# Silu of c first, gate's products beside the first pair's sums, d_skip turned behind dt, two weight differences moved

## The chip, the cores and the metric

The kernel runs on one core of one Trainium2 chip. The metric is the device time of one execution in microseconds. Three executions of the kernel before took 1301.9, 1305.21 and 1306.17 us; their median, 1305.21 us, is the time before. All times on a profile count from the start of its span.

TensorE is called PE here, VectorE DVE, ScalarE ACT, GpSimd POOL and SyncE SP. PEld is PE's weight load, which overlaps its products. SP computes nothing; its queue issues most of the loads, ACT's queue most of the stores. Each engine takes its instructions in the order in which they are written for it.

## The reference

One decoder layer runs on a prompt of 1024 rows and on 8 samples of 8 rows (64 rows), so on 1088 columns in all, with a model width of 1024:

```
mod = silu(c) @ w_ada + b_ada ; shift, scale, gate = split(mod, 3)
h = rmsnorm(x) * (1 + scale) + shift
[u_pool | z_pool | z_ssm | xBC | dt | g] = h @ w_in
P = (pool_mix(u_pool) * silu(z_pool)) @ w_pool_out
S = gated_rmsnorm(SSD(conv(xBC)) + d_skip * x, z_ssm) @ w_ssm_out
x = x + gate * ((sigmoid(g_pool) * P + sigmoid(g_ssm) * S) @ w_o)
y = rmsnorm(x, final_g)
```

`c` has nine rows: one for the prompt and one for each sample. `w_ada` is 1024 x 3072: its first 1024 columns give shift, the next scale, the last gate. Shift and scale are wanted at once, because h is made with them; gate is wanted only at the very end, when rows of y are made. `d_skip` is one number per head (32 heads) and is wanted by the SSD stage. The outputs are y for prompt and samples and the new pool, convolution and SSM states.

## The kernel before, in words

Everything is held turned: channels on the 128 partitions, the 1088 rows of x along the columns. Products are made in float32 precision by splitting each operand into a high and a low part (`whi`, `wlo`; `hh_`, `hl_`) and summing three products. Most of `h @ w_in` is done two output tiles at a time by a Strassen scheme: a *pair* is seven products, each of two halves of 272 columns, whose operands are sums of quarters of h and of w_in. The sums of h (S1, S2, S3) are made once, by `combine()`; the sums of weights are made for every pair, by `steps()` or, for the first pair, by `first_steps()`.

The change touches the opening, `first()`. There the order of the instructions of PE, ACT, DVE, POOL and SP is written out by hand and kept (`in_line`): each engine runs them as they stand in the text. Its stages are these.

- *Load and norm.* SP loads nine tiles of x (tiles 0 to 7 of 128 rows, tile 8 of the 64 sample rows), then the weights of shift and scale in two parts of eight tiles (`ada_load`: part 0 goes with h tiles 0 to 3, part 1 with 4 to 7), with raw tiles of w_in between them (`w_load`). `x_square` sums the squares of one tile on DVE or ACT, `x_root` takes the root on ACT (Sqrt table), `x_unit` takes the reciprocal and scales each x tile by it on DVE (L211).
- *Turning.* `x_turn(g3, k)` turns channel tile k of a block of x on PE and copies it out on DVE (even k) or ACT (odd k). Block 0 is x tiles 0 and 1 (256 columns), block 1 tiles 2 to 4 (384), block 2 tiles 5 to 8 (448). Block sums live in the same banks of PSUM (pools PA with three banks and PB with five).
- *Shift and scale.* `c_turn` takes Silu of c on ACT (Silu table), turns it on PE and copies it to `scT`. `ada_mm(part, k)` multiplies it with weight tile k, in four column groups of PE at once. When all eight are summed, `ada_end` copies the sum out on ACT, turns it on PE and adds the biases on DVE, into `md`. `v_turn` turns the bias vectors.
- *h and the first two output tiles.* `h_make(block, ks)` writes high and low parts of h for some channel tiles, on ACT and DVE. `products(block, ks)` multiplies them with the weights of two tiles of g by the plain scheme; `done` takes Sigmoid on ACT (Sigmoid table) and stores it.
- *dt and the first pair.* `dt_block` multiplies h by the 32 dt columns (`dtw`), three blocks of 256, 384 and 448 columns; ACT writes the result into one of the buffers `s1`, `u2`, `u3` and stores it. `done` uses the same buffers in the order s1, u2, u3, c2, s1, u2. `combine()` is a generator; each `next(sums)` issues a step on DVE and ACT: four steps of three sums each for S2, with a high part on ACT and the low part of the step before on DVE, then S3, S1 and the fourth operand. `late_loads()` loads the convolution's weights and d_skip and, at its second step, copies d_skip out on DVE (L342) and turns both on PE (L344, L345). Then the first pair (`light[0]`, z columns) runs; between its products a hook issues the next steps of the weight splits (`wst`) and of `combine()`.

Behind `first()` a list of units runs: `light[1]` (a pair of z columns), `gate_unit(0)`, `light[2]`, `gate_unit(1)`, and then sixteen heavy pairs (pool and convolution columns, with much DVE work) into which two more light pairs are woven; then ten light pairs beside the samples' SSD, the prompt's SSD beside the output products, and the tail with w_o. These later parts are ordered by priorities and by simulated times, not by hand.

`gate_unit(half)` makes 512 columns of gate: it loads eight weight tiles of 128 x 512 through four buffers of the unit stage (`GA`), multiplies them with `scT` in four column groups, two weight tiles per group, copies the four partial sums out on ACT and adds them by one more product with `sel9` (L1012), adds the bias on DVE and stores the nine rows to `gate_d` in DRAM.

Buffers that matter: `rawA` (three; raw weights of pairs, squares, the copied-out sums of shift and scale, and dtw), `raw` (three), `R` (three; c, x tile 8, later S1), `sq` (one; later S1's last tile).

## Time and profile before

| what | value |
|---|---|
| median of three executions | 1305.21 us |
| the profiled execution's own time | 1307.45 us |
| its span on the profile | 1305.4 us |
| granted TensorE clock over the span | 0.99 |
| busy time: PE, DVE, ACT, POOL | 1261.2, 899.9, 698.7, 677.9 us |
| DMA moved | 251.66 MB, mean 193 GB/s |

How to read the lines that follow. The page begins with the busy time of each engine; then the span is cut into 40 equal slices, with a digit for the busy tenths of each engine, the clock granted to PE in tenths of full speed, and the rate of DMA. A line of waits names who waited (engine, tile written, line of the program), for whom, the total in us, how often, and the longest. A line of the timeline gives the start and the duration in us, the engine (with a q behind its name: its queue, mostly issuing a DMA), the line, the operation, output and inputs, shapes, how many were merged, and in brackets the idle time of the engine ahead of it with what ended it. Where several are merged the duration is their sum; PE's is from the first start to the last modelled end. A line of a window gives the stretch, its length, the busy time and number of instructions of PE, PEld, DVE, ACT and POOL, then clock, DMA share and GB/s. A line of a group gives count, busy time, mean ns of one, and the idle time before.

### The profile page before, as it was taken

The page shows a single profiled execution, that of the slowest core. Times are in us where ns is not written, and L with a number is a line of the kernel's source. Part 1 is how long each engine was busy: PE and PEld are TensorE (multiplying, and loading weights), DVE is VectorE, ACT ScalarE, POOL GpSimd, SP SyncE. Part 2 cuts the span into 40 slices and gives each one's busy share as a digit, 9 for nine tenths or more (in the row PEclk, how much of TensorE's full clock was granted, in tenths as well). Part 3 has the DMA queues.
Part 4 walks back from the last instruction along what each step waited for, and adds up shares of the span by engine and source line. Part 5 has one row for each costly group of instructions (what it writes and reads, how often), then busy time and mean ns, then how long its engine had stood idle before and what let it go on. Part 6 is the DMA issues. An engine that isn't in the chain of part 4 may idle for free.

```text
span 1305.4 us, 26075 instructions
## 1 busy us (share of the span) xinstructions
PE 1261.2 (97%) x9575; PEld 1159.5 (89%) x9575; DVE 899.9 (69%) x1510; ACT 698.7 (54%) x1661; POOL 677.9 (52%) x564
## 2 busy tenths in 40 slices
PE   4989999999999999999999999999999999999998
PEld 3768899999999999999889899888888888999786
DVE  5676387978967888875777665477675877466533
ACT  4764336555746655545544554676987766201211
POOL 1006567877887877664344453366676756214000
PEclk8989999999999999999999999999999999999999
DMA  9428644645654644444556465999988665475621
GB/s 324 147 79 275 204 131 152 199 131 169 215 167 147 191 159 150 151 133 128 164 153 189 147 177 164 345 360 369 303 284 264 207 197 162 166 268 158 228 98 56
DMA packets 232568, 251.66 MB, mean 193 GB/s; under 512 B 31101, under 2 KB 173573, under 8 KB 232434
## 3 DMA queue, kind: packets, MB, share of 16 engines
q1 hardware_dynamic: 160308, 171.56, 41.5%
q10 hardware_dynamic: 72134, 78.45, 17.7%
q8 instruction: 76, 1.25, 0.4%
q14 instruction: 50, 0.41, 0.1%
HBM read 167.06 MB, written 83.01 MB: 192 GB/s over the span
## 4 chain that ended last, share of the span: by engine, by line
PE 48%; DVE 4%; DMA 4%; POOL 3%; issue 3%; ACT 3%; ACTq 0%; SPq 0%; POOLq 0%; DVEq 0%
PE mm L320 4%; PE mm L321 4%; PE mm L322 4%; PE ps L567 3%; PE ps L568 3%; PE ps L569 3%; PE mm L567 3%; PE mm L569 3%; PE mm L568 3%; PE ps L1831 2%; PE ps L1833 2%; PE ps L1832 2%; PE ps L1157 2%; PE ps L1373 1%; PE ps L1160 1%
## 5 line engine op out<-in xcount | busy, mean ns | idle before, releaser
L163 POOL TENSOR_TENSOR wlo<-rawA,whi 128x512 fp32r<-128x512 f32 x120 | 192.9, 1612 | 189.0 <-ACT whi L160 113.8
L163 POOL TENSOR_TENSOR wlo<-raw,whi 128x512 fp32r<-128x512 f32 x92 | 149.8, 1634 | 127.2 <-ACT whi L160 123.7
L320 PE MATMUL mm<-Y,whi 128*128 128x352 f32 (+1 forms) x480 | 164.7, 343 | 0.5 <-DVE G L1734 0.4
L321 PE MATMUL mm<-Y,whi 128*128 128x352 f32 (+1 forms) x480 | 158.6, 330 | 1.0 <-DVE Y L1408 1.0
L322 PE MATMUL mm<-Y,wlo 128*128 128x352 f32 (+1 forms) x480 | 158.2, 330 | 0.0
L567 PE MATMUL mm<-Y,whi 128*128 128x272 f32 x496 | 147.0, 296 | 0.7 <-DVE GA L583 0.4
L567 PE MATMUL ps<-Y,whi 128*128 128x272 f32 x496 | 144.6, 292 | 0.8 <-DVE h L1253 0.5
L569 PE MATMUL mm<-Y,wlo 128*128 128x272 f32 x496 | 143.1, 289 | 2.0 <-POOL wlo L163 2.0
L568 PE MATMUL mm<-Y,whi 128*128 128x272 f32 x496 | 143.1, 289 | 0.4 <-DVE Y L447 0.4
L568 PE MATMUL ps<-Y,whi 128*128 128x272 f32 x496 | 143.1, 289 | 0.0
L569 PE MATMUL ps<-Y,wlo 128*128 128x272 f32 x496 | 142.8, 288 | 0.0
L160 ACT ACTIVATE whi<-rawA 128x512 fp32r<-128x512 f32 x125 | 78.3, 627 | 106.9 <-PE ps L568 49.9
L965 DVE SCALAR_TENSOR_TENSOR GA<-GA,cvT,GA 128x1112 f32<-128x1112 f32 x72 | 129.8, 1807 | 0.0
L160 ACT ACTIVATE whi<-raw 128x512 fp32r<-128x512 f32 x96 | 58.8, 626 | 92.4 <-DVE raw L514 58.2
L567 PEld LDWEIGHTS mm<-Y,whi 128*128 128x128 f32 x496 | 93.3, 188 | 6.0 <-ACT whi L160 1.7
L320 PEld LDWEIGHTS mm<-Y,whi 128*128 128x128 f32 x480 | 91.3, 190 | 6.6 <-issue 4.3
L567 PEld LDWEIGHTS ps<-Y,whi 128*128 128x128 f32 x496 | 93.3, 188 | 4.1 <-issue 2.7
L569 PEld LDWEIGHTS mm<-Y,wlo 128*128 128x128 f32 x496 | 93.4, 188 | 2.8 <-POOL wlo L163 2.4
L568 PEld LDWEIGHTS mm<-Y,whi 128*128 128x128 f32 x496 | 93.4, 188 | 1.5 <-DVE Y L447 0.8
L568 PEld LDWEIGHTS ps<-Y,whi 128*128 128x128 f32 x496 | 93.3, 188 | 0.3 <-issue 0.2
L569 PEld LDWEIGHTS ps<-Y,wlo 128*128 128x128 f32 x496 | 93.4, 188 | 0.2 <-issue 0.2
L321 PEld LDWEIGHTS mm<-Y,whi 128*128 128x128 f32 x480 | 91.4, 190 | 1.7 <-DVE Y L1408 1.6
(448 smaller groups left out, 3780.1 us busy)
## 6 DMA issues: line engine op xcount, KB each, us to landing
rawA<-in_w_in SPq DMA_DIRECT2D x46, 512.0 KB
dec<-acs_d SPq DMA_DIRECT2D x32, 512.0 KB
xbc<-GA ACTq DMA_DIRECT2D x24, 512.0 KB
xb<-xbc SPq DMA_DIRECT2D x32, 384.0 KB
rawA<-in_w_in SPq DMA_DIRECT2D x32, 256.0 KB
pw<-in_w_ssm_out ACTq DMA_DIRECT2D x32, 256.0 KB
ws<-ph ACTq DMA_DIRECT2D x32, 256.0 KB
ws<-pw SPq DMA_DIRECT2D x32, 256.0 KB
```

What stands on the lines that cost most here:

```text
L160: ins = act(hi[:, :, :ncols], raw[:, :, :ncols], AF.Copy)
L163: (eng or nc.gpsimd).tensor_tensor(lo[:, :, :ncols], raw[:, :, :ncols], hi[:, :, :ncols].bitcast(F32), ALU.subtract)
L320: mm(ps[:, :n], a, rh[k][:, o:o + n], start=(k == 0), stop=False)
L321: mm(ps[:, :n], a, rl[k][:, o:o + n], start=False, stop=False)
L322: mm(ps[:, :n], b, rh[k][:, o:o + n], start=False, stop=(k == nk - 1))
L567: mm(p, hi, ah, start=(k == 0), stop=False)
L568: mm(p, hi, al, start=False, stop=False)
L569: mm(p, lo, ah, start=False, stop=(k == 3))
L965: V.scalar_tensor_tensor(d[:, :n], rp[:, k:k + n], cvT[:, 24 * k + mc:24 * k + mc + 1], d[:, :n], ALU.mult, ALU.add)
L1157: mm(o[hh], xd[:S, 2 * q + hh, :], dec[:S, 2 * q + hh], start=True, stop=state is None)
L1831: mm(ps[:, :cw], mhk, wo[k][0][:, s], start=(k == 0), stop=False)
L1832: mm(ps[:, :cw], mhk, wo[k][1][:, s], start=False, stop=False)
```

## The change

- Silu's table is loaded first, by the small activation that loaded Sqrt's before, now ahead of four small loads of bias vectors. `c_turn` stands behind the first two squares instead of between the turns of the third block.
- x tiles 5 and 6 are scaled on POOL instead of DVE. The square of x tile 7 on DVE and the root of tiles 5 to 7 stand behind the first four turns of block 1.
- The eight shift-and-scale products of part 0 stand between the turns of block 2, and only its last turn is behind `ada_end(0)`.
- `first_steps()` makes its first two differences (t3 and t2) in a step of their own, which runs ahead of `ada_end(1)`; for that the first pair's weights are asked for earlier on SP. `dtw` gets a buffer of its own beside the turned x.
- Gate's products are part of `first()`: eight weight tiles of 128 x 1024 in the buffers R and sq, all eight summed in one bank in four column groups of 256 columns; four behind the later `products` of blocks 0 and 1, four behind the dt blocks. The sum is copied with its bias by one DVE instruction and stored by four DMAs on SP. `gate_unit`, `sel9` and the two units are gone.
- All six `done` run before the sums; the dt blocks follow the `products` directly; the second step of `late_loads` (d_skip) stands behind the dt blocks and gate's last products.
- `light[2]` is woven among the heavy pairs, three light pairs instead of two.

```diff
--- before.py
+++ after.py
@@ -127,14 +127,14 @@
     c9 = R([NB + 1, D])
     store_(c9[0:1, :], c_prompt)
     store_(c9[1:NB + 1, :], c_sample)
+
+    act(rc[:, 0:1], eps, AF.Silu)
+    nc.gpsimd.memset(rc[:, 0:1], 1.0)
     vb = sm.tile([44, P], F32, tag="stc", name="vb", bufs=4)
     store_(vb[0:16, :], b_ada[0, 0:2048].rearrange("(m p) -> m p", p=P))
     store_(vb[16:24, :], norm_g[0].rearrange("(m p) -> m p", p=P))
     store_(vb[24:40, :], ssm_norm_g[0].rearrange("(m p) -> m p", p=P))
     store_(vb[40:44, :], pool_scale[0].rearrange("(m p) -> m p", p=P))
-
-    act(rc[:, 0:1], eps, AF.Sqrt)
-    nc.gpsimd.memset(rc[:, 0:1], 1.0)
     scT = const([P, KT, 32], "scT")
     nc.gpsimd.memset(scT, 0.0)
     vT = const([P, 44], "vT")
@@ -208,7 +208,7 @@
         n = xr[a][1]
         V.reciprocal(rs[:n, a:b], rs[:n, a:b])
         for i in range(a, b):
-            V.tensor_scalar(xr[i][0][:n], xr[i][0][:n], rs[:n, i:i + 1], None, ALU.mult)
+            (nc.gpsimd if i in (5, 6) else V).tensor_scalar(xr[i][0][:n], xr[i][0][:n], rs[:n, i:i + 1], None, ALU.mult)
 
     tf = [None] * KT
 
@@ -515,10 +515,11 @@
 
             def first_steps():
                 t3, t2 = raw_(), raw_()
+                diff(t3, b22, b12)
+                diff(t2, t3, b11, ALU.add)
+                yield
                 add(b11)
                 add(b21)
-                diff(t3, b22, b12)
-                diff(t2, t3, b11, ALU.add)
                 diff(b21, t2, b21)
                 yield
                 add(b21)
@@ -683,7 +684,7 @@
 
 
     def dt_w():
-        raw = pa.tile([P, KT, NH], F32, tag="rawA", name="dtw", bufs=3)
+        raw = tfp.tile([P, KT, NH], F32, tag="dtw", name="dtw", bufs=1)
         load(raw, w_in[0, :, C_DT:C_DT + NH].rearrange("(k p) c -> p k c", p=P))
         return raw
 
@@ -789,6 +790,32 @@
         yield 1
 
 
+    gate_d = dram("gate_d", [NB + 1, D])
+    gw, gp2 = {}, []
+
+    def gate_load(k):
+        gw[k] = hs.tile([P, D], F32, tag="sq", name=nm("gk"), bufs=1) if k % 4 == 3 else R((P, D))
+        load(gw[k], w_ada[0, k * P:(k + 1) * P, 2 * D:])
+
+    def gate_mm(k):
+        if k == 0:
+            gp2.append(PB())
+        for j in range(4):
+            mm(gp2[0][32 * j:32 * j + 32, :256], scT[:, k, :], gw[k][:, 256 * j:256 * j + 256], start=(k == 0), stop=(k == KT - 1))
+
+    def gate_bias():
+        bg = tfp.tile([P, 256], F32, tag="bg", name="bg", bufs=1)
+        nc.gpsimd.memset(bg, 0.0)
+        for j in range(4):
+            load(bg[32 * j:32 * j + NB + 1], b_ada[0, 2 * D + 256 * j:2 * D + 256 * j + 256].partition_broadcast(NB + 1))
+        return bg
+
+    def gate_end(bg):
+        V.tensor_tensor(bg, gp2[0][:, :256], bg, ALU.add)
+        for j in range(4):
+            load(gate_d[:, 256 * j:256 * j + 256], bg[32 * j:32 * j + NB + 1])
+
+
     def first():
         ET = mybir.EngineType
         every = (ET.PE, ET.Activation, ET.DVE, ET.Pool, ET.SP)
@@ -847,6 +874,7 @@
 
         x_square(0, V)
         x_square(1, V)
+        c_turn()
         x_root(0, 2)
         x_unit(0, 2)
         x_square(2, None)
@@ -861,11 +889,11 @@
             x_turn(0, k)
         x_unit(4, 5)
         x_square(5, None)
-        x_square(7, V)
         x_square(6, None)
-        x_root(5, 8)
         for k in range(4):
             x_turn(1, k)
+        x_square(7, V)
+        x_root(5, 8)
         x_unit(5, 8)
         x_square(8, None)
         x_root(8, 9)
@@ -873,23 +901,25 @@
             x_turn(1, k)
         x_unit(8, 9)
         v_turn()
-        for k in range(2):
+        ada_mm(0, 0)
+        for k in range(4):
             x_turn(2, k)
-        c_turn()
-        for k in range(2, 4):
-            x_turn(2, k)
-        for k in range(4):
-            ada_mm(0, k)
+            if k % 2:
+                ada_mm(0, 1 + k // 2)
         w_split(0, 0)
         w_split(1, 0)
-        for k in range(4, 8):
-            ada_mm(0, k)
+        ada_mm(0, 3)
         x_turn(2, 4)
+        ada_mm(0, 4)
+        x_turn(2, 5)
+        ada_mm(0, 5)
+        ada_mm(0, 6)
+        ada_mm(0, 7)
+        x_turn(2, 6)
         ada_end(0)
 
         h_make(0, range(4))
-        for k in range(5, 8):
-            x_turn(2, k)
+        x_turn(2, 7)
         products(0, range(4))
         h_make(1, range(4))
         ada_mm(1, 0)
@@ -901,28 +931,36 @@
         for k in range(2, 8):
             ada_mm(1, k)
         products(2, range(2))
+        dtw = dt_w()
+        run, (wz, wst) = light[0][1], light[0][0]()
+        bg = gate_bias()
+        for k in range(4):
+            gate_load(k)
+        next(wst)
         ada_end(1)
-        dtw = dt_w()
         products(2, range(2, 4))
 
         for bi in range(3):
             h_make(bi, range(4, 8))
         for bi in range(3):
             products(bi, range(4, 8))
-
-        run, (wz, wst) = light[0][1], light[0][0]()
+            for k in range(2 * bi, min(2 * bi + 2, 4)):
+                gate_mm(k)
+                gate_load(k + 4)
+
         next(wst)
-        for bi in range(2):
+        for bi in range(3):
             for t in range(2):
                 done(bi, t)
         sums = combine()
-        next(sums)
-        for t in range(2):
-            done(2, t)
-        next(late, None)
         for i in range(3):
             dt_block(dtw, i)
             next(sums)
+        for k in range(4, 8):
+            gate_mm(k)
+        next(late, None)
+        next(sums)
+        gate_end(bg)
         next(wst)
 
         def hook(n):
@@ -978,41 +1016,6 @@
         store_(new_conv_p[0, 0, :, mc * P:(mc + 1) * P], o27[0:3])
         store_(new_conv_s[0, :, :, mc * P:(mc + 1) * P], o27[3:27])
         yield 1
-
-
-    gate_d = dram("gate_d", [NB + 1, D])
-    sel9 = const([P, NB + 1], "sel9")
-    nc.gpsimd.tensor_tensor(sel9, ident[:, 0:9], ident[:, 32:41], ALU.add)
-    nc.gpsimd.tensor_tensor(sel9, sel9, ident[:, 64:73], ALU.add)
-    nc.gpsimd.tensor_tensor(sel9, sel9, ident[:, 96:105], ALU.add)
-
-    def gate_unit(half):
-        c = slice(2 * D + half * 512, 2 * D + half * 512 + 512)
-
-        def ws():
-            out = []
-            for j in range(4):
-                w = GA([P, 2, 512])
-                load(w, w_ada[0, 2 * j * P:(2 * j + 2) * P, c].rearrange("(k p) c -> p k c", p=P))
-                out.append(w)
-            return out
-
-        def run(w):
-            bg = GA([P, 512])[:NB + 1]
-            load(bg, b_ada[0, c].partition_broadcast(NB + 1))
-            pg = PB()
-            for kk in range(2):
-                for r in range(4):
-                    k = 4 * kk + r
-                    mm(pg[32 * r:32 * r + 32, :], scT[:, k, :], w[k // 2][:, k % 2], start=(kk == 0), stop=(kk == 1))
-            gs = pa.tile([P, 512], F32, tag="c2", name=nm("gs"))
-            act(gs, pg, AF.Copy)
-            yield
-            ps = PB()
-            mm(ps[:NB + 1, :], sel9, gs, start=True, stop=True)
-            V.tensor_tensor(bg, ps[:NB + 1, :], bg, ALU.add)
-            store_(gate_d[:, half * 512:half * 512 + 512], bg)
-        return (ws, run)
 
     H0B = 4
 
@@ -1473,8 +1476,8 @@
             load(new_pool_s[0, :, 0:7, :], state_pool[0, :, 8:15, :])
 
     first()
-    units = [plain(to_conv), light[1], gate_unit(0), light[2], gate_unit(1), plain(pool_rows)]
-    units += weave(heavy, light[3:-LAST])
+    units = [plain(to_conv), light[1], plain(pool_rows)]
+    units += weave(heavy, light[2:-LAST])
     pre = splits()
     units.append(plain(lambda: [None for _ in pre]))
     units.append(plain(to_ssd))
```

## The prediction

> **What bounds the kernel now.** I read the page's busy times and slices first, then TensorE's own waits over the first 130 us, then busy time by stage, then the timeline of the stages that the change touches.
>
> ```profile
> PE 1261.2 (97%) x9575; PEld 1159.5 (89%) x9575; DVE 899.9 (69%) x1510; ACT 698.7 (54%) x1661; POOL 677.9 (52%) x564
> ...
> PEclk8989999999999999999999999999999999999999
> ...
> GB/s 324 147 79 275 204 131 152 199 131 169 215 167 147 191 159 150 151 133 128 164 153 189 147 177 164 345 360 369 303 284 264 207 197 162 166 268 158 228 98 56
> ```
>
> PE (TensorE) is busy 97% of the span, so the time moves only where PE stands still, runs at the lower clock, or gets other work. The clock line shows both dips in the first three slices (32.6 us each). The GB/s line bounds what has landed: 324 GB/s over the first slice is 10.6 MB.
>
> ```profile
> PE ps L345 <- DVE dx L342: 3.8, 1, 3.8
> PE ps L147 <- ACT R L144: 3.0, 1, 3.0
> ```
>
> These are PE's two longest single waits of the first 130 us that the change addresses: for the turned `d_skip` (L345) and for Silu of c (L147).
>
> ```profile
> core 0: us, PE busy (x) PEld busy (x) DVE busy (x) ACT busy (x) POOL busy (x), PEclk, DMA share, GB/s
> 22.70:25.60 2.90, 0.00 (x0) 0.00 (x0) 0.00 (x0) 2.88 (x3) 0.00 (x0) 0.50 1.13 332
> 25.70:32.20 6.50, 6.50 (x48) 3.82 (x52) 0.86 (x2) 1.58 (x3) 2.08 (x2) 0.50 0.89 311
> ...
> 54.00:62.00 8.00, 7.28 (x49) 6.69 (x48) 6.02 (x17) 6.45 (x12) 0.00 (x0) 1.00 0.25 77
> ...
> 68.10:72.10 4.00, 0.16 (x1) 0.16 (x1) 3.65 (x7) 2.00 (x5) 0.00 (x0) 0.77 0.37 131
> 72.10:76.90 4.80, 4.80 (x45) 2.04 (x49) 4.50 (x9) 1.96 (x5) 0.00 (x0) 0.50 0.34 128
> 76.90:82.00 5.10, 5.10 (x60) 1.58 (x52) 4.12 (x6) 1.75 (x3) 0.00 (x0) 0.98 0.20 67
> 200.00:300.00 100.00, 100.00 (x782) 97.98 (x781) 84.79 (x122) 60.76 (x148) 77.48 (x45) 1.00 0.56 174
> ```
>
> Each row has the stretch, its length, the busy time of the five engines, granted clock, DMA share and rate. PE is idle from 22.70 to 25.60, runs to 32.20 at clock 0.50, is idle again from 68.10 to 72.10 and at 0.50 to 76.90. From 200 to 300 it has no idle time at all while DVE has 85: there, whatever is saved ahead passes through to the end.
>
> **The change part by part.** *Start.*
>
> ```profile
> 15.49 1.22 DVE L199 SCALAR_TENSOR_TENSOR sqj<-Y 128x1024 f32<-128x1024 f32 x1 [1.04 <-DMA Y<-in_x_prompt]
> ...
> 21.68 0.27 PE L222 MATMUL ps<-ident,R 64*128 64x64 f32 x1 [1.44 <-DVE R L211]
> ...
> 22.36 0.31 PE L222 MATMUL ps<-ident,R 64*128 64x64 f32 x1
> ...
> 23.26 1.28 ACT L144 ACT_TABLE_LOAD   x1
> ...
> 24.55 1.06 ACT L144 ACTIVATE R<-R 9x1024 f32<-9x1024 f32 x1
> ...
> 26.61 0.90 PE L222 MATMUL ps<-ident,Y 128*128 128x128 f32 x3
> ...
> 27.74 0.90 PE L222 MATMUL ps<-ident,Y 128*128 128x128 f32 x3
> ...
> 28.87 5.53 PE L244 MATMUL ps<-Y,scT 128*32 128x256 f32 x64
> ...
> 36.22 1.09 ACT L283 ACTIVATE Y<-tf,md 128x256 fp32r<-128x256 f32 x2 [1.35 <-DVE md L256]
> ...
> 46.97 2.80 PE L244 MATMUL ps<-G,scT 128*32 128x256 f32 x48
> ```
>
> Before, Silu's table load (1.28) and Silu (1.06) stand behind the second turn of the third block (rows 21.68 and 22.36); two more turns follow at half clock, and the first shift-and-scale product starts at 28.87, the last ends at 34.40, and the first h is written at 36.22. A turn takes 0.68 at full clock (22.36-21.68) and 1.13 at half (27.74-26.61). A shift-and-scale step of one weight tile takes 2.80/6 = 0.47 at full clock, so about 0.9 at half. All eight weight tiles are within the first 9.2 MB of the sync queue (x is 8 loads of 512 KB and one of 256, weights 8 of 512, two raws of 256), which by the rate of the first slice is there at 9.2/0.324 = 28.3 us.
>
> After, the Silu table takes the place of the first Sqrt table, Sqrt is loaded right behind Silu, so there are as many loads as before, and the first root comes between 0 and 1.28+1.06 later; I take 0.6, as most of it lies beside the first vector squares. DVE's wait for x tile 7 (1.04 in row 15.49) swallows that. That square ended at 16.7; behind the first two vector copies of the second block it ends about 1.5 later, so with root and reciprocal the scalings of tiles 5 to 7 start near 18.9. Two of the three go to POOL, where the trace has no scaling by a column. Its bounds:
>
> ```profile
> L163 POOL TENSOR_TENSOR wlo<-rawA,whi 128x512 fp32r<-128x512 f32 x120 | 192.9, 1612 | 189.0 <-ACT whi L160 113.8 <-DVE S L447 66.4 <-PE ps L1247 6.4
> ...
> L1136 POOL TENSOR_SCALAR_AFFINE_SELECT dec<-dec 128x1024 f32<-128x1024 f32 x32 | 36.0, 1125 | 23.5 <-DMA R<-gp 10.2 <-ACT cE L1341 7.1 <-DMA dec<-acs_d 6.0
> ```
>
> One input of 1024 columns took 1.12 us (L1136); two inputs of 512 took 1.61, so 1024 would take 3.2. Two tiles are ready at 21.1 or at 25.3. Nearest is L1136, one input and the same width: 21.1, before the 21.68 at which the third block started anyway, so it costs nothing; its upper end costs 3.6. The Trainium skill (GPSIMD Engine Reference, section Engine selection) says that one-input work on POOL is roughly line-rate and two-input work about twice as slow as VectorE; at the one-input rule the cost stays zero. Its specifications say that POOL shares SBUF interfaces with VectorE instructions in a two-port mode, which speaks against the edit; no run here prices that.
>
> From 21.7 PE then has six turns and seven weight steps until the part is summed: 6x0.68+7x0.47 = 7.4 us at full clock, so 29.1; 13.2 at half, so 34.9, as late as before. With a drop as at 22.3 and a recovery as at 72.10 to 76.90 (4.8 us at half, which cost 2.4) it is 31.5. I take 31.2 against 34.40: **3.2 us gained** (0 to 5.3). The split of the first two raws moves up with the turns, so the raw buffer that held the queue comes free sooner and no later load is held back.
>
> *Two weight differences.*
>
> ```profile
> 52.63 0.20 DVE L256 TENSOR_TENSOR md<-ps,vT 128x36 f32<-128x36 f32 x1 [1.16 <-PE ps L252]
> ```
>
> Two DVE instructions of 0.68 (row 67.47 below) move from behind the first pair's splits to ahead of the second part's sums of shift and scale. DVE idles there for 1.16, waiting for PE's turned sums, so 1.36 cost 0.2, taken as nothing; if the raws are late, see the rivals. `dtw` in a buffer of its own frees a `rawA`, so both raws can load at once.
>
> *Gate's first four products.* 4x0.47 = 1.9 on PE, beside 0.72 of idle time in the row 54 to 62: 1.2 lost. Its eight loads of 512 KB and four bias loads go on SP behind the pair's raws, with a DMA share of 0.25 in that row. The last four wait only for the products that free their buffers; behind them on SP stand the stores of gate, which wait for DVE's gate sum near 80, then the next pair's raws, which are needed only when the first pair's seven products are nearly through.
>
> *d_skip behind dt.*
>
> ```profile
> 66.75 1.28 ACT L830 ACT_TABLE_LOAD   x1
> ...
> 67.47 0.68 DVE L514 TENSOR_TENSOR raw<-rawA,rawA 128x512 f32<-128x512 f32 x1
> ...
> 68.05 0.39 ACT L830 ACTIVATE g<-mm 128x256 f32<-128x256 f32 x1
> ...
> 68.88 0.38 ACT L830 ACTIVATE g<-mm 128x256 f32<-128x256 f32 x1 [0.44 <-ACT g L830]
> ...
> 69.53 0.72 DVE L466 TENSOR_TENSOR tf<-tf,tf 128x544 f32<-128x544 f32 x1
> ...
> 78.91 1.68 PE L697 MATMUL mm<-Y,dtw 128*32 128x448 f32 x16
> ...
> 82.02 0.39 PE L567 MATMUL mm<-Y,whi 128*128 128x272 f32 x1
> ...
> 634.78 0.34 ACTq L681 DMA_DIRECT2D z<-u  x1
> ...
> 638.25 0.44 DVE L578 TENSOR_TENSOR u<-s,mm 128x272 f32<-128x272 f32 x1 [1.78 <-DMA z<-u]
> ```
>
> PE idles 68.1 to 71.9 on DVE's copy of d_skip, and two thirds of dt run at half clock. The last dt block (448 columns) took 82.02-78.91 = 3.11 at full clock; all 1088 columns then take 7.6. With 3.2 gained and 1.2 lost PE ends the block products at 66.1, dt at 73.7, gate's last four products (1.9) at 75.6. That would be 6.4 before 82.02. What is late next is the d_skip copy: DVE has it behind three steps of sums, and the second and third hold a low part that waits for ACT's high part, which stands behind the dt evacuation. That one writes the buffer of the fifth Sigmoid, whose store must land. In numbers: Sigmoids start at 68.05-3.2 = 64.9, one per 0.85, so the fifth's store leaves at 69.0; a store took 3.5 from issue to its reader in the rows at 634.78 and 638.25. Then dt 0.5, gap 0.4, high part 0.7, low part 0.7, three sums (0.72 each), low part 0.7, copy 0.2, turn 0.3: 78.1. With a landing that nobody waits for PE sets it: 75.6. The DMA share is 0.37 or less here (rows 68.10 and 72.10), so I take a landing a little quicker than that, 77.4: the first product of the pair starts **4.6 us** before 82.02 (0.5 to 6.4). This contains the start's gain and all of gate's new PE work.
>
> The Trainium skill (TensorE: Matmul & The Clock Gate, Part 1) says that an idle window of about 3.4 us halves the clock and a busy one restores it, on a free-running window. The trace agrees: 3.85 idle, then 0.50 for 4.8 us. By it the wait left, below 2.5 us, keeps full clock, as I assume.
>
> *Gate units gone.*
>
> ```profile
> 152.25 1.92 PE L1007 MATMUL ps<-GA,scT 128*32 128x512 f32 x16
> 154.10 0.40 PE L567 MATMUL mm<-Y,whi 128*128 128x272 f32 x1
> ...
> 157.57 1.03 PE L1012 MATMUL ps<-gs,sel 128*9 128x512 f32 x2
> 158.53 0.39 PE L567 MATMUL ps<-Y,whi 128*128 128x272 f32 x1
> ```
>
> One half took PE 154.10-152.25 and 158.53-157.57: 1.85+0.96 = 2.81; two halves **5.6 us**, saved whole, since PE has no idle time behind. Also gone are their 4 MB of loads there, two ACT evacuations, and on POOL three tiny sums. The third light pair goes among the heavy ones. Three light pairs spread over sixteen heavy ones instead of two: runs of heavy pairs get shorter, and PE was fully busy in longer ones, so nothing (-3 to +4 for other phases of later waits).
>
> Sum: 4.6+5.6 = 10.2 against the profiled run of 1307.45 (span 1305.4 and 2.05 around it): 1297.2. That run lies 2.2 above the median; against 1305.21 I predict 1295.
>
> **The rivals.** (1) The start gives nothing: PE at half clock throughout, or POOL at 3.2 per tile, or the last weights late. For it: the clock did fall at 22. Against: PE now has unbroken work. 3.2 less: 1298.2. (2) The d_skip copy is only moved into a longer chain on DVE: S2 late by 4 more takes back nearly all of 4.6: 1299. For it: the in-order queue above; against: it needs a landing of over 7 us. (3) Slower: DVE stands in line at the two differences until both raws are there.
>
> ```profile
> 41.73 11.30 SPq L500 DMA_DIRECT2D rawA<-in_w_in  x2
> ```
>
> Before, the second load could leave only at 53 (11.30 for two). After, the queue ahead of them is 15.1 MB, by 0.324 there at 46.6 and needed at 48.0 (52.63, less 3.2, less the two themselves). Each us later delays the second half of h, one for one; 10.2 late is no change, over 14 late is slower: 1310. That requires the second load to wait for a buffer and gate's weights to pass it; SP is in order and gate's loads stand behind. (4) Other waits take it back: of PE's 44 us of idle time (1305.4-1261.2) a part lies in later stages, where its phase moves, and could grow by 8; 1303. Against: the row from 200 to 300.
>
> **How the numbers follow.** Forecast 0.62; (1) 0.15; (2) 0.08; (3) 0.05; (4) 0.10. About 0.3% (3.9 us) is what a measurement of this kernel can tell from no change: faster below 1301.3, slower above 1309.1. The forecast, (1) and (2) are faster, 0.85 in all, of which 0.02 stray to no change; (4) is no change but for 0.01; (3) is slower. So 0.83, 0.11, 0.06. The forecast's own range is 1289 (start 5.3, no wait at d_skip, 2 from later waits) to 1300. To leave out 2 in 10 it runs to 1303, and 1288 below for the scatter of the runs.
>
> **What would show it.** Last part-0 product near 31; PE's wait at L345 below 2.5; dt at clock 1.00 in under 8 us; first pair's first product near 77; the second pair at once followed by the heavy one without gate products. Wrong if the differences wait on DMA, if POOL's scalings last over 2 us each, or if PE's idle time behind 100 us grows by more than 4.

## The result, and the profile after

Twenty executions of the changed kernel have a median of 1303.34 us (1301.43 to 1307.35), twenty of the kernel before, on the same chips, 1304.76 (1301.77 to 1309.53). The ratio is 0.9988 with a 95% interval of 0.9979 to 0.9998: a gain of about 0.1%, where 0.8% was forecast, and just above the range's upper end of 1303. The profiled execution of the changed kernel took 1303.16 us with a span of 1301.4, so it lies at its median, while the profiled execution of before lies 2 to 3 us above its own. Of the 4.2 us between the ends of the two traces less than half is therefore in the medians.

First the head of the page of the changed kernel: busy times, then granted clock of PE in 40 slices of 32.5 us.

```profile
PE 1260.4 (97%) x9603; PEld 1162.7 (89%) x9603; DVE 888.8 (68%) x1507; ACT 698.3 (54%) x1659; POOL 681.0 (52%) x564
...
PEclk8999999999999999999999999999999999999999
```

The second dip (the 8 in the third slice of before) is gone; the first stayed. PE's waits over the first 130 us (who waited, for whom, total, times, longest) and the timeline of the opening say why.

```profile
PE ps L147 <- ACT R L144: 6.4, 1, 6.4
PE ps L222 <- POOL Y L211: 3.9, 2, 2.3
...
PE ps L345 <- DVE dx L342: 0.8, 1, 0.8
```

```profile
19.15 6.22 POOL L211 TENSOR_SCALAR Y<-Y,rs 128x1024 f32<-128x1024 f32 x2 [15.78 <-DVE rs L209]
...
22.14 11.50 SPq L828 DMA_DIRECT2D raw<-in_w_in  x2
...
25.42 0.69 PE L222 MATMUL ps<-ident,Y 128*128 128x128 f32 x2 [2.34 <-POOL Y L211]
...
35.67 1.50 PE L244 MATMUL ps<-Y,scT 128*32 128x256 f32 x24
...
38.99 1.09 ACT L283 ACTIVATE Y<-tf,md 128x256 fp32r<-128x256 f32 x2 [1.37 <-DVE md L256]
```

The two scalings on POOL took 6.22 us, 3.1 each on average, and ended at 25.37; the prediction's own sign of being wrong was over 2 us each. PE waited for the first and again for the second, and could turn the third block in earnest only from 25.42. The last shift-and-scale products of part 0 ended at 37.17 (before: 34.40) and the first h is written from 38.99 (before: 36.22). The two raw loads on SP wait for a buffer that the late turns hold back, so the weights of part 1 behind them are asked for only at 33.69. The 6.4 us wait at L147 is the first 6.4 us of the span, in which PE has nothing else to do.

Windows of the changed kernel (stretch, length, busy time of PE, PEld, DVE, ACT, POOL, clock, DMA share, GB/s):

```profile
21.80:25.40 3.60, 0.48 (x1) 0.18 (x1) 0.77 (x1) 0.00 (x0) 3.57 (x2) 0.50 1.10 337
25.40:35.20 9.80, 9.78 (x53) 4.65 (x54) 1.88 (x3) 2.12 (x4) 2.74 (x3) 0.50 0.65 213
...
42.14:45.55 3.41, 3.41 (x16) 3.33 (x16) 1.86 (x5) 3.38 (x7) 0.00 (x0) 0.50 1.10 339
...
66.00:73.70 7.70, 7.70 (x51) 6.35 (x49) 6.90 (x15) 6.50 (x11) 0.00 (x0) 1.00 0.64 223
73.70:81.30 7.60, 7.60 (x101) 3.28 (x104) 4.32 (x8) 3.20 (x6) 0.00 (x0) 1.00 0.49 169
200.00:300.00 100.00, 98.82 (x775) 96.89 (x774) 82.14 (x120) 61.16 (x150) 81.46 (x47) 1.00 0.56 182
```

After the idle stretch PE is busy for 9.8 us at half clock, and it falls to half once more from 42.14 to 45.55, which the trace of before does not show. From 66 on the picture is the one forecast: the products run into dt without a gap, and dt runs in 7.5 us at full clock. What follows dt, and what it waits for:

```profile
78.21 0.47 ACT L701 ACTIVATE dts<-mm,dtb 128x256 f32<-128x256 f32 x1 [1.06 <-DMA gs<-g]
...
79.77 0.73 DVE L462 TENSOR_TENSOR Y<-tf,Y 128x544 fp32r<-128x544 f32 x1 [3.14 <-ACT Y L469]
...
81.50 0.58 ACT L701 ACTIVATE dts<-mm,dtb 128x384 f32<-128x384 f32 x1 [1.76 <-DMA gs<-g]
...
83.82 0.21 DVE L342 COPY dx<-dk 16x128 f32<-16x128 f32 x1
...
84.08 0.23 PE L345 MATMUL ps<-ident,dx 16*128 16x16 f32 x1 [0.81 <-DVE dx L342]
84.24 0.39 PE L568 MATMUL mm<-Y,whi 128*128 128x272 f32 x1
```

The chain is the predicted one: ACT's dt evacuation (its copy of dt out of PSUM) waits for a store of the fifth Sigmoid (and, a step later, the sixth), ACT's high part stands behind it, DVE waits 3.14 us for that, and the copy of d_skip comes last. It costs PE 0.81 us.

### The profile page after: what moved, and what is told of

The parts are those of the page before. It is cut to its first block, busy times and chain, and to the rows that moved or that the text cites. A ratio compares the mean times of both kernels' runs of the same rounds, so it can differ in the third digit from the quotient of the medians.

```text
span 1301.4 us, 26116 instructions
## 1 busy us (share of the span) xinstructions
PE 1260.4 (97%) x9603; PEld 1162.7 (89%) x9603; DVE 888.8 (68%) x1507; ACT 698.3 (54%) x1659; POOL 681.0 (52%) x564
## 4 chain that ended last, share of the span: by engine, by line
PE 54%; issue 8%; POOL 5%; DMA 5%; DVE 4%; ACT 3%; SPq 0%; ACTq 0%; POOLq 0%; DVEq 0%
PE ps L568 5%; PE ps L569 5%; PE ps L570 5%; PE mm L568 5%; PE mm L570 5%; PE mm L569 5%; PE mm L320 3%; PE mm L321 3%; PE mm L322 3%; PE ps L1834 2%; PE ps L1835 2%; PE ps L1836 2%; PE ps L1160 1%; POOL G L1743 1%; PE ps L1376 1%
## 5 line engine op out<-in xcount | busy, mean ns | idle before, releaser
L163 POOL TENSOR_TENSOR wlo<-rawA,whi 128x512 fp32r<-128x512 f32 x120 | 184.0, 1538 | 188.8 <-ACT whi L160 108.1
```

Source lines behind the costliest of these rows:

```text
L163: (eng or nc.gpsimd).tensor_tensor(lo[:, :, :ncols], raw[:, :, :ncols], hi[:, :, :ncols].bitcast(F32), ALU.subtract)
```

## The experiments

All differences of trace positions below are against the trace of before. They were read from the timelines at the same products; "first pair" is the start of its first product, "fourth pair" the first after the place where the gate units stood, "end of pairs" the end of the last product ahead of the samples' SSD, "end" the end of PE's last product. The trace of before took 1307.45 us, 1.1 to 3.6 above the medians of before that stand beside these runs (1303.87 to 1306.37), so a single position that differs by this much says little. Of the labels, e1_dve and e1_again are the first experiment below, run twice; p_ marks one part put alone into the kernel before, l_ the changed kernel with VectorE's scalings and a part left out.

```
trace position, us      first h   dt      first   fourth  end of  end
                        products  begins  pair    pair    pairs
before                  37.27     72.16   82.02   154.10  830.17  1299.16
after                   +2.37     +1.61   +2.23   -2.10   -2.37   -4.22
e1_dve                  -1.95     -4.22   -3.72   -8.77   -9.87   -9.95
e1_again                -4.38     -5.22   -4.95   -9.99   -8.93   -7.77
l_nostart               -1.66     -4.02   -4.01   -8.36  -10.55   -9.36
p_pool                  +2.73     +2.67   +1.96   +1.67   +3.66   +1.72
p_start                 -2.67     -1.54   -2.64   -2.46   -1.23   -3.71
p_dskip                 -1.52     -5.19   -3.95   -3.30   -0.12   -1.93
l_nogate                -1.81     -4.32   -3.06   -0.59   -0.46   -1.62
p_gate                  -2.37     +3.95   +5.29   -0.96   -1.56   -0.58
```

**VectorE instead of POOL for tiles 5 and 6.** The theory was that POOL's scalings are what took the gain; the rival that the gain was lost elsewhere.

```diff
-            (nc.gpsimd if i in (5, 6) else V).tensor_scalar(xr[i][0][:n], ...)
+            V.tensor_scalar(xr[i][0][:n], ...)
```

> The changed kernel with x tiles 5 and 6 scaled on DVE again. Theory (POOL's scaling, 3.1 us per tile, is what lost the start): the third block's turns begin near 22.5 instead of 25.4, the first h is written at 34 to 36 instead of 38.99, the second pair's end moves by as much, and the time falls by 3 to 5 us below the changed kernel's 1303.3, to about 1299. Rival (PE's half clock sets the start whatever POOL does): the first h stays at 37.5 or later and the time stays within 1.5 us of 1303.3.

Measured: 1296.69 us against 1306.25 of before, ratio 0.9913 (0.9888 to 0.9938). The same kernel once more, on another chip:

> e1_dve again beside e5_copies, for a comparison on one chip: 1296.7 by its first measurement; the sum of my parts with POOL's price taken out would be 1295.

Measured: 1299.51 against 1306.37, ratio 0.9952 (0.9932 to 0.9972). Timeline of the first of them, then the same window of the first and of the second:

```profile
18.43 2.08 DVE L211 TENSOR_SCALAR Y<-Y,rs 128x1024 f32<-128x1024 f32 x3
...
21.03 0.90 PE L222 MATMUL ps<-ident,Y 128*128 128x128 f32 x3
...
31.35 1.50 PE L244 MATMUL ps<-Y,scT 128*32 128x256 f32 x24
...
34.68 1.09 ACT L283 ACTIVATE Y<-tf,md 128x256 fp32r<-128x256 f32 x2 [1.37 <-DVE md L256]
```

```profile
20.01:30.25 10.24, 9.83 (x56) 4.60 (x60) 3.89 (x10) 2.41 (x5) 1.97 (x2) 0.50 1.07 368
```

```profile
20.01:30.25 10.24, 8.19 (x88) 4.27 (x88) 5.24 (x12) 3.77 (x9) 2.76 (x3) 1.00 1.07 367
```

Three scalings on DVE take 2.08 together, 0.7 each, and turning resumes at 21.03. With one line put back the kernel is 6.9 to 9.6 us below before, of the forecast 10.2; the theory had expected 3 to 5 us from this line and got more. In the first trace the last products of part 0 end at 32.85: the clock is at half for 10.24 us although PE is busy for 9.83 of them. In the second trace the same kernel runs this stretch at full clock throughout, and these products end at 30.42. So how long half clock lasts here is not a property of the kernel. The second drop at 42.14 of the changed kernel is not POOL's doing either: the kernel with the late dt evacuation (below) keeps POOL's scalings and does not have it, and the second trace here, without them, has one from 35.13 to 38.54.

**What POOL's operations cost.** The kernel above with twelve POOL instructions added, two of each form, into a scratch tile that nothing reads. Its one execution, 1311.17 us, is used for the prices alone.

```diff
         x_unit(0, 2)
+        for _ in range(2): nc.gpsimd.tensor_scalar(scr[:, :D], xs0[:, :D], rs[:, 0:1], None, ALU.mult)
+        for _ in range(2): nc.gpsimd.tensor_scalar(scr[:, :D], xs0[:, :D], 1.5, None, ALU.mult)
+        ... (512 columns; copy; two-input multiply at 1024 and at 512)
```

> As e1_dve, with twelve extra POOL instructions on a scratch tile ahead of POOL's first split, to price them: scaling 1024 columns by a column, by a constant, 512 columns by a column, copying 1024, multiplying two inputs of 1024 and of 512. If one-input work costs what the 1024-column selection did (1.1 us), the copy and both scalings take 1.0 to 1.3. If the column operand is what costs, the scaling by a column takes 3.1 and the constant 1.1. If every arithmetic scaling costs it, both take 3.1 and the copy 1.1.

The groups of POOL by form, 5 to 40 us (count, busy us, mean ns of one):

```profile
L885 POOL TENSOR_SCALAR scr<-Y 128x1024 f32<-128x1024 f32 x2 | 6.9, 3454 | 0.2
L883 POOL TENSOR_SCALAR scr<-Y,rs 128x1024 f32<-128x1024 f32 x2 | 6.4, 3214 | 5.9 <-DVE Y L211 5.8
L891 POOL TENSOR_TENSOR scr<-Y 128x1024 f32<-128x1024 f32 x2 | 3.8, 1892 | 0.2
L887 POOL TENSOR_SCALAR scr<-Y,rs 128x512 f32<-128x512 f32 x2 | 3.7, 1868 | 0.2
...
L889 POOL COPY scr<-Y 128x1024 f32<-128x1024 f32 x2 | 2.1, 1038 | 0.1
```

Scaling 1024 columns takes 3.2 us by a column and 3.5 by a constant on average; a copy of the same tile takes 1.04, and a two-input multiply (of a tile with itself) 1.89. A rival is that DVE, which was at work beside the scalings and not beside the copies, slowed POOL down. The trace of the changed kernel settles it (POOL, then DVE, from 22.6 to 27 us):

```profile
22.53 2.84 POOL L211 TENSOR_SCALAR Y<-Y,rs 128x1024 f32<-128x1024 f32 x1
```

```profile
26.45 0.63 DVE L228 COPY tf<-ps 128x448 f32<-128x448 f32 x1 [3.87 <-PE ps L222]
```

DVE was idle for 3.87 us up to 26.45, and the second of POOL's scalings, which lies in that time but for its first 0.05, still took 2.84; the first, beside a busy DVE, took 3.40. So most of the price belongs to scaling as POOL does it, not to the column as second operand and not to DVE; the 0.56 more of the first came beside DVE's work. DVE is slower there too: its scalings of tiles 5 to 7 took 2.89 us beside POOL's added work, against 2.08 without it.

**POOL's scalings alone, on the kernel before.**

```diff
-            V.tensor_scalar(xr[i][0][:n], ...)
+            (nc.gpsimd if i in (5, 6) else V).tensor_scalar(xr[i][0][:n], ...)
```

> The kernel before with x tiles 5 and 6 scaled on POOL and nothing else. POOL is done near 24 (3.1 us each from 17.8), the third block's turns wait for it, but before the change they were followed by Silu's wait to 25.7 anyway. Theory (POOL's price counts only where nothing else stands): first product of h 0 to 2 us later, time 0 to 2 us above before. Rival (the price is paid wherever it is put): 4 us or more above.

Measured: 1309.45 against 1303.87, ratio 1.0041 (1.0025 to 1.0056). PE's waits over the first 130 us have one new line:

```profile
PE ps L222 <- POOL Y L211: 4.4, 2, 2.5
```

5.6 us of median for two instructions: taken out of the changed kernel they gave back 5.4 to 8.1 (from 1.4 below before to 6.9 and 9.6), put into the kernel before they cost 5.6. The rival's figure came. Silu's wait hides nothing, because ACT takes Silu only behind its copy of the third block's second turn, which is now late: Silu's table load starts at 26.52 instead of 23.26, and PE waits the same 3.0 us for it afterwards.

**The new opening alone.** The order of `first()` up to the first `products`, and Silu's table first; all nine scalings on DVE.

```diff
+        c_turn()                    # behind the first two squares
...
+        ada_mm(0, 0)
+        for k in range(4):
             x_turn(2, k)
-        c_turn()
+            if k % 2:
+                ada_mm(0, 1 + k // 2)
```

> The kernel before with the opening's new order alone (Silu first, part-0 products among the third block's turns, square of tile 7 later), all scalings on DVE. Theory (my term of 3.2 us for the start was right without POOL): first product of h 2 to 3.5 us earlier than 37.27 and the time 2 to 4 us below the kernel before. Rival (ACT and DVE pace h whatever comes ahead): under 1 us.

Measured: 1305.28 against 1303.87, ratio 1.0010 (0.9996 to 1.0024). The trace is 2.67 us early at the first products of h and 2.64 at the first pair, as the theory had it, but nothing of that is in the time. Two things bear on it. First, the trace of before is a poor base for this stretch: the kernels whose opening is the old one to the letter or nearly so had the first products of h at 37.27 (before), 35.75, 34.91 and 35.61, those of six traces with the new opening and no scaling on POOL at 34.60, 35.33, 34.36, 32.89, 35.47 and 32.92. The means are 35.9 and 34.3, so the new opening is worth 1.6 at that place, not 3.2. Most of the difference inside one group is the clock: windows of 30 to 34 us, of before and then of the kernel of the d_skip part (below), which has the same opening:

```profile
30.00:34.00 4.00, 4.00 (x52) 1.91 (x48) 0.00 (x0) 0.56 (x2) 2.50 (x2) 0.66 0.70 192
```

```profile
30.00:34.00 4.00, 4.00 (x61) 2.32 (x53) 0.40 (x1) 0.44 (x2) 2.13 (x2) 0.98 0.66 155
```

The Trainium skill (TensorE: Matmul & The Clock Gate, Part 1) says that the window which decides on the clock runs freely, so that the same program changes clock at other places from run to run; this pair of rows agrees, and so do the two traces of one kernel above (0.50 and 1.00 over the same stretch).

Second, a later wait grows. PE's waits from 590 to 700 us, of before, then of this kernel:

```profile
PE mm L569 <- POOL wlo L163: 0.9, 1, 0.9
```

```profile
PE mm L568 <- POOL wlo L162: 1.9, 2, 1.7
```

The wait for POOL's low part grew by 1.0, and the lead of 2.46 at the fourth pair is 1.23 at the end of the pairs. But the same trace ends 3.71 early, and its execution (1303.72) lies 1.6 below this kernel's median, so that later waits took the rest is not shown.

**The opening undone in the good version.** The changed kernel with VectorE's scalings and the old opening.

> The changed kernel with the opening put back as it was (all nine scalings on VectorE). Theory (gains carried through): the new opening is worth 2.6 us, so the time is 2 to 3 us over the changed kernel with VectorE's scalings (ratios 0.9913 and 0.9952), that is a ratio of about 0.996, with the fourth pair near 148 us. Rival (the parts only pay together, by where the later waits fall): ratio 0.999 or more although the fourth pair is early.

Measured: 1298.10 against 1304.65, ratio 0.9953 (0.9937 to 0.9969). The expected ratio came, but not for the reason given: with the new opening the ratios were 0.9913 and 0.9952, so at most one of the two shows it to be worth anything. The dt blocks begin at 68.13 here and at 67.94 and 66.94 with the new opening. The fourth pair at 145.74, where the theory had it near 148, says that the other parts carry the gain. Of these, gate's part and d_skip are looked at below; the two weight differences were never run apart.

**d_skip behind dt alone.**

```diff
-        for bi in range(2):
+        for bi in range(3):
             for t in range(2):
                 done(bi, t)
         sums = combine()
-        next(sums)
-        for t in range(2):
-            done(2, t)
-        next(late, None)
         for i in range(3):
             dt_block(dtw, i)
             next(sums)
+        next(late, None)
+        next(sums)
```

> The kernel before with d_skip turned behind dt and all six Sigmoids ahead of the sums, nothing else. Theory (the stall of 3.85 and the half clock behind it go, and a wait of 0.8 to 2.5 for d_skip's copy comes): dt in under 8 us at clock 1.00, the first pair's first product 3.5 to 5 us before 82.02, time 3 to 5 us below. Rival (the wait only moves to DVE's copy): under 1.5 us.

Measured: 1304.60 against 1303.87, ratio 0.9998 (0.9978 to 1.0018). PE in the timeline:

```profile
72.80 1.69 PE L697 MATMUL mm<-G,dtw 128*32 128x448 f32 x16
...
77.87 0.26 PE L345 MATMUL ps<-ident,dx 16*128 16x16 f32 x1 [3.13 <-DVE dx L342]
...
78.92 0.43 PE L567 MATMUL mm<-Y,whi 128*128 128x272 f32 x1
...
82.40 0.29 PE L568 MATMUL ps<-Y,whi 128*128 128x272 f32 x1
```

dt is at full clock and ends 7.60 early. But the wait is only moved behind it: 3.13 us instead of 3.8, and now the first product of the pair runs at half clock (0.43 for one instruction of 272 columns instead of 0.29). Of 7.60 remain 3.95 at the first pair and 2.50 at the second, and the pairs end 0.12 early.

**Opening and d_skip together, without gate's part** (and without the two weight differences).

> The kernel before with the new opening (all nine scalings on VectorE) and d_skip behind dt, but with the gate units left where they were. Theory (gains of the parts are carried through): the opening alone had the pairs 2.6 us earlier and d_skip alone 3.3 us at the fourth pair, so together the fourth pair starts near 148 us instead of 154.1, the time is some 5 us below before, ratio about 0.996. Rival (each later wait takes back what comes early, unless the gate units are gone): the fourth pair is early in the trace, but the early start shrinks pair by pair to under 2 us at the end of the pairs, and the ratio is 0.999 to 1.001, as for either part alone.

Measured: 1305.47 against 1304.65, ratio 1.0010 (0.9991 to 1.0030). The rival's ratio, but the early start does not shrink pair by pair: the loss sits at one place, as in the run before: a wait of 3.1 us behind dt, then the window from 66 to 84 us at a mean clock of 0.82, and from a lead of 3.06 at the first pair 0.59 is left at the second. Window of this kernel, then of the one with gate's part and the old opening:

```profile
66.00:84.00 18.00, 14.39 (x127) 9.31 (x126) 15.42 (x26) 9.64 (x18) 0.00 (x0) 0.82 0.40 131
```

```profile
66.00:84.00 18.00, 17.79 (x189) 12.04 (x188) 14.16 (x24) 10.18 (x21) 0.00 (x0) 1.00 0.36 125
```

With gate's four products behind dt PE works for 17.79 of 18 us at full clock; its wait for the turned d_skip is 0.21 there. The two kernels differ in the two weight differences as well, but these do not move the copy that PE waits for. DVE's copy of d_skip, in the kernel with d_skip's part alone and then in the one with gate's part and the old opening:

```profile
77.61 0.21 DVE L342 COPY dx<-dk 16x128 f32<-16x128 f32 x1
```

```profile
77.58 0.21 DVE L343 COPY dx<-dk 16x128 f32<-16x128 f32 x1
```

The copy comes at the same time; what fills PE's wait is gate's eight products, the first four of which move dt back by about 1.2 and the last four of which take about 1.9 behind it.

**Gate's part alone.** Gate's products in the opening, the two units gone, d_skip and opening as before.

> The kernel before with gate's products in the opening and the two gate units gone, nothing else. Theory (5.6 us of PE go, 3.8 come at full clock, about 0.7 of them in idle time): first pair up to 3.8 later, fourth pair 1.8 to 2.5 earlier, time 1.8 to 2.5 us below. Rival (gate's loads or its bank hold back the first pair): no gain.

Measured: 1306.67 against 1303.87, ratio 1.0022 (1.0008 to 1.0036). I had put gate's loads ahead of the first pair's on SP, and so this run shows the part together with a late raw (timelines of PE, ACT and SP):

```profile
75.90 0.28 PE L345 MATMUL ps<-ident,dx 16*128 16x16 f32 x1 [8.37 <-DVE dx L342]
```

```profile
68.61 0.63 ACT L160 ACTIVATE whi<-rawA 128x512 fp32r<-128x512 f32 x1 [5.29 <-DMA rawA<-in_w_in]
```

```profile
56.67 5.70 SPq L797 DMA_DIRECT2D R<-in_w_ada  x3
...
62.90 0.97 SPq L500 DMA_DIRECT2D rawA<-in_w_in  x2
```

It is close to rival (3): gate's second loads wait on SP for R to come free, the raws behind them keep ACT waiting for 5.29 us, DVE's d_skip copy stands behind the raws' low parts, and PE waits 8.37 instead of 3.8. The first pair is 5.29 late. By the fourth pair that is -0.96: 6.25 won in between, so the units' 5.6 are real. The changed kernel asks for the raws ahead of gate's loads and escapes this. That the median is 2.8 over before although the pairs end 1.56 early in the trace is mostly the base: the trace of before took 1307.45, 3.6 above its median of 1303.87 here, while this kernel's took 1306.79, at its own median. The 6.25 did no more than make up for the late start.

**The dt evacuation behind the sums step.** In the changed kernel ACT writes dt out behind its high part instead of ahead of it.

```diff
-            dt_block(dtw, i)
+            evacuate = dt_block(dtw, i)
             next(sums)
+            evacuate()
```

> The changed kernel with each dt block's evacuation on ACT put behind the step of sums that follows it, so that S2's high parts no longer stand behind the Sigmoid stores. Theory (DVE's wait for S2's high parts is 3.1 us, but PE waited only 0.8 for the d_skip copy): DVE's longest wait at L462 falls below 1, the first pair's product starts 0.8 earlier and the pair itself is up to 1.2 shorter: 1 to 2 us in all. Rival (DVE sets nothing here): under 0.5 us.

Measured: 1301.89 against 1306.25, ratio 0.9966 (0.9952 to 0.9981). PE's wait for the copy is gone:

```profile
80.52 0.23 PE L345 MATMUL ps<-ident,dx 16*128 16x16 f32 x1
80.68 0.40 PE L568 MATMUL mm<-Y,whi 128*128 128x272 f32 x1
```

The stretch from dt's end to the first pair went from 2.95 to 2.07 us, nearly all of it gate's products and the two turns. The first pair itself kept its length of 24.55 (24.59 in the changed kernel, 23.34 before), and DVE's longest wait at L462 is 1.6, where the theory had it below 1. So the first half of the theory came, 0.88 us, and the second did not; the rest of the difference in time is not shown to come from this edit, as the opening of this trace was 1.2 earlier too.

**VectorE's scalings, the evacuation behind the sums and d_skip copied ahead of them, all in one**, and then also the copies of the turned d_skip and convolution weights behind the fourth sums:

```diff
+        next(late)                  # dx copied ahead of the sums (e4)
         sums = combine()
...
         ps = PB()                   # late_loads, second step
...
+        yield                       # e5: copies behind the fourth sums
         V.tensor_copy(cvT, ps[:, :120])
```

> e1_dve and e3_evac together, and the d_skip copy on DVE ahead of all sums (its turn on PE stays behind gate's last products). If the losses found in the trace add up (3 to 5 at the start, 1 to 2 behind dt), the time is 1297 to 1299, some 6 to 8 us below the kernel before; if one only hides the other, 1300 or more.

Measured: 1296.88 against 1306.25, ratio 0.9923 (0.9902 to 0.9944); the first pair starts at 75.11 and takes 24.56.

> e4_all with DVE's two copies of the turned convolution weights and d_skip behind the fourth step of sums and gate's sum, so that DVE does not wait for PE there. Theory (the first pair's sixth product waits 1.2 us longer than before because DVE comes to S1 that much later): the sixth product takes 3.7 instead of 4.9, the first pair 23.3 to 23.6 instead of 24.56, the time 1 us below e4_all's 1296.9. Rival (ACT's order sets S1): the first pair stays at 24.5.

Measured: 1296.80 against 1306.37, ratio 0.9946 (0.9926 to 0.9966); the pair's sixth product takes 3.73 instead of 4.9 and the pair 23.35, as before the change. This settles the 1.2 us by which the first pair got longer: DVE's two copies and the fourth sums stand ahead of the sums (S1) that the sixth product reads. In the time neither version can be told from VectorE's scalings alone (0.9923 beside 0.9913 on one chip, 0.9946 beside 0.9952 on another).

## Why the prediction was wrong

*Start: this step failed, by the price of POOL's scaling.* The text bounded it between 1.12 and 3.2 us for one tile, took the lower end because one-input work of the same width (L1136) was the nearest row, and so set its cost to nothing. It was 3.1, with the two tiles ready at 25.4: the upper end almost to the tenth (25.3). The nearest row was the wrong one: that operation is a select, and its time says nothing of a scaling, as the added instructions show with copies at 1.04, two-input multiplies at 1.89 and scalings at 3.2. The upper end's cost was also too small: 3.6 by the text, 5.6 measured alone and 5.4 to 8.1 in the changed kernel. Most of that is there at the first products of h: with POOL's scalings they start at 40.00 with the old opening, 4.1 behind its mean, and at 39.65 and 38.49 with the new one, 4.8 behind its mean on average. PE's two waits for the tiles fall in a stretch at half clock or just ahead of it, and that stretch lasts 13.65, 13.65 and 10.24 us in these three traces, against 0 to 10.24 in the others. What makes up the rest of the cost in time stays open. The one-input rule of the Trainium skill (GPSIMD Engine Reference, section Engine selection: roughly line-rate) pointed to the same wrong end; the runs agree with it for a copy and contradict it for a scaling by a factor of nearly three.

*Start, the rest: the base was too slow, not the new opening.* Without POOL's delay the last products of part 0 end between 30.42 and 33.00 in the six traces of the new opening, 31.8 on average, where the text took 31.2. But they end at 34.40 only in the one trace of before that was at hand; in the other three traces of the old opening they end at 32.88, 32.03 and 32.74. So against the mean of the old openings 1.2 were gained there instead of 3.2, and 1.6 at the first products of h. The recovery of the clock was taken from the row at 72.10 as 4.8 us; half clock lasted 6.83 there, as it began at 70.25 with PE idle, and in the opening it lasted from nothing to 10.24 without POOL's delay. That 31.2 lies so near the average is luck in part, as single traces lie up to 1.4 off it. In the time the opening showed no gain of its own, neither alone (1.0010) nor as the part undone (0.9953 without it). The raw buffer, which was to come free sooner, did so only with VectorE's scalings.

*Two weight differences: right as far as the trace shows.* They were never run apart. Rival (3) did not come in the changed kernel: in its timeline both run without a wait for DMA.

```profile
53.73 0.69 DVE L514 TENSOR_TENSOR raw<-rawA,rawA 128x512 f32<-128x512 f32 x1
54.45 0.69 DVE L514 TENSOR_TENSOR raw<-raw,rawA 128x512 f32<-128x512 f32 x1
```

That its mechanism exists is shown by the run with gate's part alone, where the raws were late.

*Gate's first four products: right.* With the old opening and all else, dt begins at 68.13, with d_skip's move alone at 66.97; 1.16 between them, 1.2 forecast. The first products of h start within 0.14 of each other in these two traces; the 1.16 contains whatever the two weight differences cost.

*d_skip behind dt: right in its mechanism, its cover underrated.* dt at full clock took 7.5 us (7.6 forecast), the wait left was 0.81 (below 2.5) and the clock stayed full behind it, the order of what is late next came as told: store, evacuation, high part, low part, copy. The first pair at 84.24 is 6.8 behind the forecast 77.4, but it starts at 78.30, 77.06 and 78.00 in the three runs without POOL's delay that keep gate's part and this step as they are. What the text did not see is that gate's four products, which it booked as a cost, are what fills the wait: without them the same chain leaves PE idle for 3.13 us and half clock falls on the pair. Nor does a wait below 2.5 keep full clock as a rule: 2.15 us of idle time ended at 20.02 in the first trace of VectorE's scalings, with half clock behind it. And it let the copies behind the turn go for nothing; they cost the first pair 1.2.

*Gate units gone: right.* Between the first pair's end and the fourth pair the changed kernel wins 5.57 (from +3.47 at the second pair to -2.10), 5.6 forecast, and it stays to the end of the pairs (-2.37). The new weave of the light pairs, set at nothing, is in every run without the units and was not priced apart.

*The rivals.* (1) named the mechanism, POOL at 3.2 for a tile, and its time of 1298.2 was 5 too low by the undersized price. (2) did not come: the chain was there, but the Sigmoids' stores held ACT for 1.06 and 1.76 us only, and PE for 0.81. (4) gave the time that was measured, but not by its mechanism. By the busy times of the windows 100 to 830 and 830 to 1300 us PE idles for 15.7 us from 100 us to its last product in before and for 17.2 in the changed kernel; it grew by 1.5, not by the 4 that the text set as its limit, and a little of it is the first pair's. The stretch from 200 to 300, which had no idle time in before, has 1.18 us in the changed kernel.

The sum with the measured terms: 10.2 forecast, less 5.6 for POOL, less 1.6 for the opening's smaller gain (1.6 instead of 3.2) and 1.2 for the longer first pair, leaves 1.8; the medians differ by 1.4. Without POOL's term it is 7.4, where 6.9 and 9.6 were measured. That it closes so well is luck in part: POOL's term is known only as 5.4 to 8.1, and the opening's gain does not show in the time. Why the parts alone sum to nothing is settled in the traces for d_skip (without gate's products behind dt its wait only moves) and not settled for the opening.

## What to carry to other kernels

A price that no row shows, between ends a factor of three apart, must be carried at the end that hurts when the operation stands ahead of the bounding engine; moving two instructions of 0.7 us to a slower engine cost over half of all that the other edits won together. When a wait is moved, put other work of the waiting engine into its new place: the same edit left PE idle for 3.13 us and the next pair at half clock when nothing stood behind dt, and 0.2 to 0.8 us at full clock with four products there. Before a stage is priced from one trace, look how much that stage differs between kernels that share it; here two traces of one kernel lay 2.4 us apart at the first products of h, one with 10.24 us of half clock ahead of them and one with none.

## What was not expected of the hardware

- On POOL, scaling a float32 tile of 1024 columns took 2.8 to 3.8 us, by a column or a constant alike, more than a two-input multiply (1.89) and three times a copy (1.04); at 512 columns 1.87. On DVE the same scaling took 0.7. With DVE idle beside it POOL's took 2.84.
- An idle time of PE of 3.13 us was enough for half clock in the products behind it (0.43 instead of 0.29); in another trace half clock began behind one of 2.15 us.
- Half clock came in whole steps of 3.41 us: in the first 130 us of every trace of this case that has any, its stretches are 3.41, 6.83, 10.24 or 13.65 us long. The rows from 20.01 and 42.14 above are two of them; two more are the opening of the changed kernel and, before the change, the wait for d_skip:

```profile
21.66:35.31 13.65, 10.36 (x55) 4.87 (x55) 2.76 (x5) 2.12 (x4) 6.45 (x5) 0.50 0.78 249
```

```profile
70.25:77.08 6.83, 5.14 (x45) 2.35 (x49) 6.25 (x12) 2.93 (x6) 0.00 (x0) 0.50 0.38 142
```

- A busy PE did not always end it after one step: over 20.01 to 30.25 PE was busy for 9.83 of 10.24 us at half clock. The traces don't show why.
